# Weight loads: a list that shares both DMA queues by the packet, and a sixth place for raw weights

## The chip, the cores and the metric

The kernel runs on one core of one Trainium2 chip. The metric is device time in microseconds (us) of one execution; a profile of one execution comes from the hardware profiler.

## The reference, cut to what matters

```python
def swiglu(x, w_in, w_out):
    gate, up = jnp.split(x @ w_in, 2, axis=-1)
    return (jax.nn.silu(gate) * up) @ w_out
...
for layer in range(DEPTH):                       # DEPTH = 2
    h = h + 0.5 * swiglu(rms_norm(h, ffn1_norm[layer]), ffn1_w_in[layer], ffn1_w_out[layer])
    hn = rms_norm(h, mix_norm[layer])
    # layer 0: stick-breaking attention; layer 1: sliding-window attention with sinks, on a shared K/V
    h = h + attention(hn) @ w_o
    h = h + 0.5 * swiglu(rms_norm(h, ffn2_norm[layer]), ffn2_w_in[layer], ffn2_w_out[layer])
return rms_norm(h, final_norm)
```

All arrays are float32. There are 256 tokens, the model width is 1024, and each of the four feed-forward nets (FFNs) has a hidden width of 2816, so that one FFN reads a w_in of 1024 x 5632 and a w_out of 2816 x 1024. The weights are read once, and there are many of them for few tokens.

## The kernel before, in words

A float32 product is made from three cheaper ones: each operand is split into a high part, rounded to the type fp32r, and the remainder. For weights this is `split` (L419, L421): ScalarE (ACT) writes w_hi by a copy, and VectorE (DVE) writes w_lo = raw - w_hi, in two pieces of 128 x 1024 for each weight tile of 1 MB. TensorE (PE) then takes w_hi twice and w_lo once (`step`, `mm` L288). The operands on the other side are called xT (the normed stream), S (sums of quarters of it) and aT (the hidden activations) in the names that follow.

Tiles of raw weights live in five places (`RAWS = 5`) of a ring called `RAW`. A load into a place can only start when the last reader of the weights before it, mostly a w_lo on DVE, is done. All plain loads go through SyncE's queue (SP, L369), in order. The split halves live in ten places of `WP`.

An FFN is cut into blocks of hidden columns. Most of them (kind "s", `strassen`) compute the gate and up halves for both 128-token tiles with seven products in place of eight. Such a block loads four tiles r11, r12, r22 and r21, adds r12 and then r22 into r11 on DVE (L611), and has two more tiles added by the DMA engines themselves: `fetch` (L616) issues an accumulating transfer from GpSimd's queue (POOL), once into r12, and once into r11, after the product that uses r11 + r12 + r22 has been split. The last product of the block, on xT, needs this last fetch. Its gate result goes through a silu on ACT and a multiplication on DVE (L789, tile m), is transposed on PE (L677), and becomes aT. The w_out products of the block before (called out here) are done between the products of the block, and at the end of an FFN the products of the last two blocks follow one another.

No order is written by hand. The kernel builds a list of tasks with durations and dependencies (`Plan`), and `listed` runs through it engine by engine: among the tasks that are ready, each engine takes the one with the smallest priority. `due` works back from the end to give each task a due time, which is its priority in the next of four passes (PE keeps the given one), and the best pass sets the order of every engine's queue. In this model a plain load occupies SP for its bytes divided by 283 to 375 bytes per ns, one load after the other, and is usable 2000 ns later; a fetch takes 1500 ns of POOL, and SP for its bytes divided by 170.

Norm weights lie in two places `G4` of 512 KB. 8192 bytes are set aside as descriptor scratch of POOL's transfers.

Of the kernel before, what the change touches and what calls it, by code (L numbers as in the profile page):

```python
# [17 lines left out]
P = 128  # L18
# [19 lines left out]
PAIRS = 5  # L38
RAWS = 5
# [41 lines left out]
HEAD = 700.0  # L81
PASSES = 4
# [5 lines left out]
class Task:  # L88
    __slots__ = ("eng", "dur", "fn", "prio", "deps", "outs", "left", "ready", "start", "end", "seq", "lat")

    def __init__(self, eng, dur, fn, prio, seq, lat):
        self.lat = lat
# [23 lines left out]
class Plan:  # L116
# [3 lines left out]
    def add(self, eng, dur, fn, r=(), w=(), prio=None, lat=None):  # L120
# [19 lines left out]
        t.deps.discard(t)  # L140
        self.tasks.append(t)
        return t

    def lag(self, t, o):
        return t.lat if t.lat is not None else 0.0 if o.eng == t.eng and t.eng != "SP" else LAT[t.eng]

    def listed(self, prio):
        free = {e: HEAD for e in LAT}
        wait = {e: [] for e in LAT}
        queue = {e: [] for e in LAT}  # L150
        for t in self.tasks:
            t.ready, t.left = 0.0, len(t.deps)
            if t.left == 0:
                heapq.heappush(wait[t.eng], (t.ready, t.seq, t))
        done = []
        while True:
            best = None
            for e in LAT:
                if queue[e]:
                    at = free[e]  # L160
                elif wait[e]:
                    at = max(free[e], wait[e][0][0])
                else:
                    continue
                if best is None or at < best[0]:
                    best = (at, e)
            if best is None:
                break
            at, e = best
            while wait[e] and wait[e][0][0] <= at:  # L170
                t = heapq.heappop(wait[e])[2]
                heapq.heappush(queue[e], (prio[t.seq], t.seq, t))
            t = heapq.heappop(queue[e])[2]
            t.start = at
            free[e] = at + t.dur
            t.end = at + t.dur
            done.append(t)
            for o in t.outs:
                o.ready = max(o.ready, t.end + self.lag(t, o))
                o.left -= 1  # L180
                if o.left == 0:
                    heapq.heappush(wait[o.eng], (o.ready, o.seq, o))
        assert len(done) == len(self.tasks)
        return done, max(t.end for t in done)

    def due(self, done):
# [5 lines left out]
        for t in sorted(done, key=lambda t: (-t.start, -t.seq)):  # L192
            due[t.seq] = min([last.get(t.seq, 1e18)] + [due[o.seq] - self.lag(t, o) - t.dur for o in t.outs])
# [34 lines left out]
def kernel(  # L228
# [33 lines left out]

    RAW, WP, A4 = Slots("raw", RAWS, 8), Slots("w", 2 * PAIRS, 8), Slots("a", 4, 4)
    STG, S8, G4 = Slots("stg", 6, 3), Slots("s", 2, 8), Slots("g", 2, 4)
# [103 lines left out]
    def dma(src, dst, nbytes, w, prio, r=()):  # L368
        T("SP", nbytes / (283.0 if prio < -8.5e5 + 50 else 375.0 if prio < -8e5 else PLAIN), lambda: nc.sync.dma_start(out=dst(), in_=src), r=r, w=w, prio=prio)  # L369
# [245 lines left out]
    def fetch(dst, src):  # L615
        T("POOL", 1500, lambda: nc.gpsimd.dma_start(out=dst.ap, in_=src, accum_op=ALU.add), w=[(dst, 0), (dst, 1)],  # L616
          prio=plan.pos - LOADS, lat=500.0)
        T("SP", P * 2048 * 4 / ADDING, lambda: None, w=[(dst, 0), (dst, 1)], prio=plan.pos - LOADS)
# [9 lines left out]
    def ffn(w_in, w_out, acc, rest, finish, kv=None, blocks=BLOCKS, roots=None, ending=False, there=False, arranged=False):  # L628
# [145 lines left out]
        def strassen(n, c, between):  # L774
# [54 lines left out]
            if ORD[0] == "3":  # L829
                third()  # L830
            if not early:
                second(C11)
            if ORD[0] == "2":
                third()
            product(a, r11, of_s(1), False, False)
            fetch(r11, col(0, 1, c))
            u2 = stage(a, "u2")
            if ORD[0] == "6":
                third()
            plus(u2, d)  # L840
            mul_less(lambda: s1.ap, lambda: s1.ap, lambda: u2.ap, B(u2), B(s1), 0)
            STG.put(u2)
# [671 lines left out]
    def last(t, pair):  # L1514
# [44 lines left out]
        for j, c, ks in ((0, slice(0, 320), (0,)), (1, cuts[1], (640,)), (0, slice(320, 640), (0, 512))):  # L1559
# [8 lines left out]
            T(by, 500, lambda j=j, c=c, now=now, q=nc.scalar if by == "ACT" else nc.sync: q.dma_start(out=out[0, ts(t), c], in_=hg[j].ap[:, now]),  # L1568
              r=[(hg[j], ("to", c.start))], prio=1e9)
# [42 lines left out]
```

## Time and profile before

| What | Value |
|---|---|
| Median of 3 runs (lowest, highest) | 923.02 us (922.31, 923.92) |
| The profiled execution, and its span from first to last instruction | 924.5 us, 922.7 us |
| Mean granted TensorE clock | 0.997 |
| DMA | 214.43 MB, mean 232 GB/s |
| Plain loads of 1 MB of w_in from SP | 76, median 8.7 us from issue to landing |

The profile names a group of instructions by line, engine, and out<-in. PE is matmuls and PEld the loads of their stationary operand, which run one ahead of the matmuls. A row of waits says who waited, for whom, and then the total, the number and the longest wait in us. A row of windows gives, for one stretch, the length, and then the busy time of each engine with its number of instructions, the granted clock, the mean busy share of the 16 DMA engines, and GB/s. By time, the stages are: FFN 1 of layer 0 up to about 172 us, stick-breaking attention up to 300, FFN 2 of layer 0 up to 475, FFN 1 of layer 1 up to 660 (its last block from 620 on), sliding-window attention up to 740, and FFN 2 of layer 1 up to 905.

### The profile page before, as it was taken

The numbers are of one execution on the slowest core, as the hardware profiler recorded it, in microseconds if no ns is written. First come the engines' busy times: TensorE is split into PE (matmuls) and PEld (weight loads), VectorE is DVE, ScalarE is ACT, GpSimd is POOL, SyncE is SP. The second block draws the span as 40 slices with busy tenths as digits, with TensorE's granted clock in tenths as the row PEclk, the third lists the DMA queues.
The fourth block names the chain that finished last, engine by engine and source line by source line (L and its number), as shares of the span: only waits on it lengthen the run. The fifth ranks groups of instructions, "written<-read, shape, count | busy, mean of one in ns | idle before, by whom it ended". The sixth has DMA issues, their size and how long they took to land.

```text
span 922.7 us, 11848 instructions
## 1 busy us (share of the span) xinstructions
PE 905.2 (98%) x4420; PEld 739.5 (80%) x4420; DVE 816.6 (89%) x989; ACT 646.3 (70%) x935; POOL 66.8 (7%) x71
## 2 busy tenths in 40 slices
PE   9999999999999999999999999999999999999997
PEld 6888888788888877778788887887897787787776
DVE  8989898787967999898889999987789799999887
ACT  7867566777987865685588667755868676668563
POOL 2001010000000101010001001100000010001000
PEclk9999999999999999999999999999999999999999
DMA  9897999896752699989795999999843269998981
GB/s 336 302 255 191 299 300 244 260 267 190 242 183 92 138 272 273 242 261 258 206 337 156 246 255 260 288 280 244 305 151 115 92 146 259 303 230 250 302 220 46
DMA packets 107305, 214.43 MB, mean 232 GB/s; under 512 B 6256, under 2 KB 27760, under 8 KB 107248
## 3 DMA queue, kind: packets, MB, share of 16 engines
q1 hardware_dynamic: 85184, 170.49, 52.7%
q0 software_dynamic: 21648, 42.99, 27.1%
q8 instruction: 34, 0.56, 0.2%
q10 hardware_dynamic: 416, 0.20, 0.1%
q14 instruction: 23, 0.19, 0.1%
HBM read 212.62 MB, written 1.05 MB: 232 GB/s over the span
## 4 chain that ended last, share of the span: by engine, by line
PE 41%; DVE 24%; DMA 19%; issue 10%; ACT 6%; POOL 0%; ACTq 0%; POOLq 0%; DVEq 0%; SPq 0%
PE ps L288 38%; DMA raw<-in_ffn_w_in_dram 18%; DVE w_lo L421 15%; ACT w_hi L419 5%; DVE raw L611 4%; PE ps L491 1%; DVE aT_l L498 1%; PE ps L677 1%; PE ps L1346 1%; DMA raw<-in_ffn_w_out_dram 1%; DVE s L587 0%; DVE S_l L581 0%; DVE u L786 0%; DVE xT L498 0%; DVE p L786 0%
## 5 line engine op out<-in xcount | busy, mean ns | idle before, releaser
L421 DVE TENSOR_TENSOR w_lo<-raw,w_hi 128x1024 fp32r<-128x1024 f32 x424 | 498.3, 1217 | 52.9 <-ACT w_hi L419 51.7
L419 ACT CAST w_hi<-raw 128x1024 fp32r<-128x1024 f32 x424 | 424.4, 1050 | 141.5 <-DMA raw<-in_ffn_w_in_dram 69.8
L288 PE MATMUL ps<-w_hi,xT 128*128 128x512 f32 (+1 forms) x788 | 231.6, 378 | 1.9 <-ACT w_hi L419 1.8
L288 PEld LDWEIGHTS ps<-w_hi,xT 128*128 128x128 f32 x788 | 143.0, 190 | 28.9 <-ACT w_hi L419 2.9
L288 PE MATMUL ps<-w_lo,xT 128*128 128x512 f32 (+1 forms) x394 | 148.4, 377 | 2.1 <-DVE w_lo L421 2.0
L288 PE MATMUL ps<-w_hi,aT_h 128*128 128x512 f32 x354 | 140.0, 396 | 0.0
L288 PE MATMUL ps<-w_lo,aT_h 128*128 128x512 f32 x354 | 137.7, 389 | 0.0
L288 PE MATMUL ps<-w_hi,aT_l 128*128 128x512 f32 x354 | 137.4, 388 | 0.0
L288 PE MATMUL ps<-w_lo,S_h 128*128 128x512 f32 x320 | 126.1, 394 | 1.4 <-DVE w_lo L421 1.3
L288 PE MATMUL ps<-w_hi,S_h 128*128 128x512 f32 x320 | 126.2, 394 | 0.1
L288 PE MATMUL ps<-w_hi,S_l 128*128 128x512 f32 x320 | 124.7, 390 | 0.0
L611 DVE TENSOR_TENSOR raw<-raw 128x1024 f32<-128x1024 f32 x78 | 93.7, 1218 | 1.0 <-DMA raw<-in_ffn_w_in_dram 0.8
L288 PEld LDWEIGHTS ps<-w_lo,xT 128*128 128x128 f32 x394 | 74.5, 189 | 18.4 <-DVE w_lo L421 5.1
L616 POOL DMA_DIRECT2D raw<-in_ffn_w_in_dram x38 | 48.1, 1266 | 517.6 <-ACT w_hi L419 209.2
L288 PEld LDWEIGHTS ps<-w_lo,aT_h 128*128 128x128 f32 x354 | 66.5, 188 | 14.1
L288 PEld LDWEIGHTS ps<-w_hi,aT_l 128*128 128x128 f32 x354 | 66.6, 188 | 12.9
L288 PEld LDWEIGHTS ps<-w_hi,aT_h 128*128 128x128 f32 x354 | 66.5, 188 | 12.8
L288 PEld LDWEIGHTS ps<-w_lo,S_h 128*128 128x128 f32 x320 | 60.0, 188 | 18.6 <-DVE w_lo L421 6.2
L288 PEld LDWEIGHTS ps<-w_hi,S_h 128*128 128x128 f32 x320 | 60.1, 188 | 12.2 <-ACT u L782 0.5
L288 PEld LDWEIGHTS ps<-w_hi,S_l 128*128 128x128 f32 x320 | 60.1, 188 | 12.1
L497 ACT CAST aT_h<-ps 128x512 fp32r<-128x512 f32 (+1 forms) x48 | 26.3, 547 | 56.1 <-PE ps L677 56.1
L288 PE MATMUL ps<-xT,w_hi 128*128 128x512 f32 (+1 forms) x136 | 47.0, 395 | 0.0
(184 smaller groups left out, 942.3 us busy)
## 6 DMA issues: line engine op xcount, KB each, us to landing
raw<-in_ffn_w_in_dram SPq DMA_DIRECT2D x76, 1024.0 KB, 8.7
raw<-in_ffn_w_out_dram SPq DMA_DIRECT2D x44, 1024.0 KB, 6.4
raw<-in_ffn_w_in_dram POOLq DMA_DIRECT2D x38, 1024.0 KB, 9.3
raw<-in_sb_w_qkv_dram SPq DMA_DIRECT2D x12, 1024.0 KB, 8.8
raw<-in_ffn_w_in_dram SPq DMA_DIRECT2D x16, 512.0 KB, 6.6
raw<-in_ffn_w_in_dram SPq DMA_DIRECT2D x16, 256.0 KB, 5.5
raw<-in_sb_w_o_dram SPq DMA_DIRECT2D x4, 1024.0 KB, 5.7
raw<-in_swa_w_q_dram SPq DMA_DIRECT2D x4, 1024.0 KB, 9.1
```

Source lines behind the costliest of these rows:

```text
L288: PE.matmul(ps, lhsT=lhsT, rhs=rhs, start=start, stop=stop, skip_group_check=True)
L419: T("ACT", act(m), lambda sl=sl: ACT.copy(out=flat(hi)[:, sl], in_=flat(raw)[:, sl]), r=[(raw, i) for i in rs] + first, w=[(hi, i) for i i ...
L421: T("DVE", dve(m), lambda sl=sl: DVE.tensor_sub(out=flat(lo)[:, sl], in0=flat(raw)[:, sl], in1=flat(hi)[:, sl].bitcast(F32)), r=[(raw, i) ...
L491: PE.matmul(bank.ap[:, i * P:(i + 1) * P], lhsT=s, rhs=ident, start=i == 0, stop=True, is_transpose=True, skip_group_check=True)
L497: T("ACT", act(n), lambda: ACT.copy(out=hi[2](), in_=src()), r=B(bank), w=[hi[0:2]])
L498: T("DVE", dve(n), lambda: DVE.tensor_sub(out=lo[2](), in0=src(), in1=hi[2]().bitcast(F32)), r=B(bank) + [hi[0:2]], w=[lo[0:2]])
L611: T("DVE", dve(m), lambda sl=sl: DVE.tensor_add(out=flat(dst)[:, sl], in0=flat(dst)[:, sl], in1=flat(src)[:, sl]), r=[(src, k) for k in ks ...
L616: T("POOL", 1500, lambda: nc.gpsimd.dma_start(out=dst.ap, in_=src, accum_op=ALU.add), w=[(dst, 0), (dst, 1)], prio=plan.pos - LOADS, lat=5 ...
L677: PE.transpose(out=tr.ap[:, i * P:(i + 1) * P], in_=m.ap[:, i * P:(i + 1) * P], identity=ident)
L1346: PE.matmul(z[par].ap[:, i_ * P:(i_ + 1) * P], lhsT=e.ap[:, par * 384 + c:par * 384 + c + P], rhs=ident, start=i_ == 0, stop=True, is_tran ...
```

## The change

The list now plays both DMA queues as queues of packets. A DMA task occupies its issuing engine for 500 ns (SP) or 1000 ns (POOL); 1200 or 1700 ns after its start its packets are in queue HW or SW; the heads of both queues share the 16 engines packet by packet, in proportion to the time of one packet; and a transfer ends 900 or 500 ns after its last packet. The packets' times are a table. `RAW` gets a sixth place of 8 KB per partition. 4 KB of that come from the norm weights (`G4` from two places to one), and 4 KB from the descriptor scratch (8192 to 4096 bytes). `SEED1` is False, so that the branch it guards is not taken; PAIRS = 5 becomes HL = 10, which is the same number of places.

```diff
-PAIRS = 5
-RAWS = 5
+HL = 10
+RAWS = 6
+SEED1 = False
...
+SETUP = {"HW": 1200.0, "SW": 1700.0}
+LANDS = {"HW": 900.0, "SW": 500.0}
+ISSUE = 500.0
+PACKET = {4096: 157.0, 2048: 84.0, 1024: 50.0}
+ADDED = 176.0
...
+        while events or queues["HW"] or queues["SW"]:
+            heads = {k: q[0] for k, q in queues.items() if q}
+            total = sum(h[2] for h in heads.values())
+            next_ = [(last + h[1] * total / h[2], k) for k, h in heads.items()]
...
+                    k, n, each = t.moves
+                    queues[k].append([t, n * each + (0.0 if heads else RAMP), each])
...
-    STG, S8, G4 = Slots("stg", 6, 3), Slots("s", 2, 8), Slots("g", 2, 4)
+    STG, S8, G4 = Slots("stg", 6, 3), Slots("s", 2, 8), Slots("g", 1, 4)
...
     def dma(src, dst, nbytes, w, prio, r=()):
-        T("SP", nbytes / (283.0 if prio < -8.5e5 + 50 else 375.0 if prio < -8e5 else PLAIN), lambda: nc.sync.dma_start(out=dst(), in_=src), r=r, w=w, prio=prio)
+        size = max(p for p in PACKET if p == 1024 or p <= 4 * src.shape[-1])
+        T("SP", ISSUE, lambda: nc.sync.dma_start(out=dst(), in_=src), r=r, w=w, prio=prio, moves=("HW", nbytes / size / 16, PACKET[size]))
...
     def fetch(dst, src):
-        T("POOL", 1500, lambda: nc.gpsimd.dma_start(out=dst.ap, in_=src, accum_op=ALU.add), w=[(dst, 0), (dst, 1)],
-          prio=plan.pos - LOADS, lat=500.0)
-        T("SP", P * 2048 * 4 / ADDING, lambda: None, w=[(dst, 0), (dst, 1)], prio=plan.pos - LOADS)
+        T("POOL", 1000, lambda: nc.gpsimd.dma_start(out=dst.ap, in_=src, accum_op=ALU.add), w=[(dst, 0), (dst, 1)],
+          prio=plan.pos - LOADS, moves=("SW", P * 2048 * 4 / 2048 / 16, ADDED))
...
-    nc = _bacc.Bacc("TRN2", target_bir_lowering=False, num_devices=1, dynamic_dma_scratch_size=8192)
+    nc = _bacc.Bacc("TRN2", target_bir_lowering=False, num_devices=1, dynamic_dma_scratch_size=4096)
```

The number of instructions of each kind on PE, DVE, ACT and POOL stays; their order moves. On DVE, this is the last block of FFN 2 of layer 0 before. raw_3427 is r11, raw_3491 r22, raw_3472 r21; m_3509 belongs to the block before, and the two rows of w_lo_3563 are the split after which the last fetch into r11 may be issued:

```order
L611 TENSOR_TENSOR raw_3427<-raw_3427,raw_3449 128x1024 x2
L421 TENSOR_TENSOR w_lo_3504<-raw_3427,w_hi_3494 128x1024 x2
L789 SCALAR_TENSOR_TENSOR m_3509<-p5_3329,small_67,m_3509 128x512
L421 TENSOR_TENSOR w_lo_3527<-raw_3472,w_hi_3515 128x1024
L611 TENSOR_TENSOR raw_3427<-raw_3427,raw_3491 128x1024
L421 TENSOR_TENSOR w_lo_3527<-raw_3472,w_hi_3515 128x1024
L611 TENSOR_TENSOR raw_3427<-raw_3427,raw_3491 128x1024
L421 TENSOR_TENSOR w_lo_3563<-raw_3427,w_hi_3551 128x1024
L421 TENSOR_TENSOR w_lo_3572<-raw_3491,w_hi_3536 128x1024
L421 TENSOR_TENSOR w_lo_3563<-raw_3427,w_hi_3551 128x1024
```

Before, that split ends seven instructions of 128 x 1024 behind m. The same place on DVE now, where raw_3298 is r11, raw_3371 r22, raw_3397 r21, and w_lo_3518 the split that frees r11 for the last fetch:

```order
L642 TENSOR_TENSOR raw_3298<-raw_3298,raw_3352 128x1024 x2
L452 TENSOR_TENSOR w_lo_3440<-raw_3088,w_hi_3424 128x1024
L452 TENSOR_TENSOR w_lo_3476<-raw_3298,w_hi_3460 128x1024 x2
L642 TENSOR_TENSOR raw_3298<-raw_3298,raw_3371 128x1024 x2
L529 TENSOR_TENSOR aT_l_3502<-ps_66,aT_h_3438 128x4x128
L452 TENSOR_TENSOR w_lo_3509<-raw_3397,w_hi_3474 128x1024
L452 TENSOR_TENSOR w_lo_3518<-raw_3298,w_hi_3507 128x1024 x2
L819 SCALAR_TENSOR_TENSOR m_3527<-p5_3344,small_67,m_3527 128x512
L452 TENSOR_TENSOR w_lo_3509<-raw_3397,w_hi_3474 128x1024
```

It now ends right ahead of m: m has moved behind the additions and the split. On PE, just ahead of the last product of the same block (w_hi_3668 with xT), before; the last nine of the out matmuls in front of it are shown, 15 more stand between them and the product on the fetched r12, and nine ahead of that product:

```order
L288 MATMUL ps_66<-w_hi_3577,aT_h_3422 128x512
L288 MATMUL ps_66<-w_hi_3577,aT_l_3433 128x512
L288 MATMUL ps_66<-w_lo_3599,aT_h_3422 128x512
L288 MATMUL ps_66<-w_hi_3577,aT_h_3422 128x512
L288 MATMUL ps_66<-w_hi_3577,aT_l_3433 128x512
L288 MATMUL ps_66<-w_lo_3599,aT_h_3422 128x512
L288 MATMUL ps_66<-w_hi_3577,aT_h_3422 128x512
L288 MATMUL ps_66<-w_hi_3577,aT_l_3433 128x512
L288 MATMUL ps_66<-w_lo_3599,aT_h_3422 128x512
L288 MATMUL ps_66<-w_hi_3668,xT_163 128x512 x2
```

So 33 out matmuls stood between the product on r11 + r12 + r22 with r22's own and the last one. PE at the same place now, from the last matmul of the product on the fetched r12 to the last product (w_hi_3636 with xT):

```order
L318 MATMUL ps_66<-w_lo_3569,S_h_2566 128x512
L707 MATMUL ps_66<-ident_68,s1_3595 128x128 x4
L318 MATMUL ps_66<-w_hi_3600,aT_h_3438 128x512
L318 MATMUL ps_66<-w_hi_3600,aT_l_3502 128x512
L318 MATMUL ps_66<-w_lo_3606,aT_h_3438 128x512
L318 MATMUL ps_66<-w_hi_3600,aT_h_3438 128x512
L318 MATMUL ps_66<-w_hi_3600,aT_l_3502 128x512
L318 MATMUL ps_66<-w_lo_3606,aT_h_3438 128x512
L318 MATMUL ps_66<-w_hi_3600,aT_h_3438 128x512
L318 MATMUL ps_66<-w_hi_3600,aT_l_3502 128x512
L318 MATMUL ps_66<-w_lo_3606,aT_h_3438 128x512
L318 MATMUL ps_66<-w_hi_3636,xT_176 128x512 x2
```

Nine out matmuls stand ahead of it, and the other 24 come after it. In the last block of the other FFNs the number goes from 18 to 9 (FFN 1 of layer 0), from 33 to 9 (FFN 1 of layer 1) and from 36 to 9 (FFN 2 of layer 1). SP loads the same tiles; in the opening the two halves of the second token tile of x come after the second and the third quarter tile of weights, where both came after the fourth.

More of the change, by code (lines that the diff above doesn't have):

```diff
@@ L140, in add @@
         t.deps.discard(t)
+        t.moves = moves
         self.tasks.append(t)
@@ L144, in lag, with at, begin, ended @@
     def lag(self, t, o):
-        return t.lat if t.lat is not None else 0.0 if o.eng == t.eng and t.eng != "SP" else LAT[t.eng]
+        return 0.0 if t.moves else t.lat if t.lat is not None else 0.0 if o.eng == t.eng else LAT[t.eng]
     def listed(self, prio):
         free = {e: HEAD for e in LAT}
-        wait = {e: [] for e in LAT}
-        queue = {e: [] for e in LAT}
+        ready = {e: [] for e in LAT}
+        events, made = [], [0]
+        queues, last, done = {"HW": deque(), "SW": deque()}, 0.0, []
+        def at(time, what, t):
+            made[0] += 1
+            heapq.heappush(events, (time, made[0], what, t))
+        def begin(e, now):
+            if ready[e] and free[e] <= now:
+                t = heapq.heappop(ready[e])[2]
+                t.start = now
+                free[e] = now + t.dur
+                done.append(t)
+                at(free[e], "free", t)
+                if t.moves:
+                    at(now + SETUP[t.moves[0]], "moves", t)
+                else:
+                    at(free[e], "end", t)
+        def ended(t, now):
+            t.end = now
+            for o in t.outs:
+                o.ready = max(o.ready, now + self.lag(t, o))
+                o.left -= 1
+                if o.left == 0:
+                    at(max(o.ready, HEAD), "ready", o)
         for t in self.tasks:
@@ L153, in listed @@
             if t.left == 0:
[L154 to L157, printed above, removed]
-            for e in LAT:
[L159 to L182, printed above, removed]
+                at(HEAD, "ready", t)
+        while events or queues["HW"] or queues["SW"]:
+            heads = {k: q[0] for k, q in queues.items() if q}
+            total = sum(h[2] for h in heads.values())
+            next_ = [(last + h[1] * total / h[2], k) for k, h in heads.items()]
+            over = min(next_) if next_ else (1e18, None)
+            now = min(over[0], events[0][0] if events else 1e18)
+            for h in heads.values():
+                h[1] -= (now - last) * h[2] / total
+            last = now
+            if over[0] <= now:
+                t = queues[over[1]].popleft()[0]
+                at(now + LANDS[over[1]], "end", t)
+                continue
+            while events and events[0][0] <= now:
+                _, _, what, t = heapq.heappop(events)
+                if what == "moves":
+                    k, n, each = t.moves
+                    queues[k].append([t, n * each + (0.0 if heads else RAMP), each])
+                elif what == "end":
+                    ended(t, now)
+                elif what == "ready":
+                    heapq.heappush(ready[t.eng], (prio[t.seq], t.seq, t))
+            for e in LAT:
+                begin(e, now)
         assert len(done) == len(self.tasks)
@@ L192, in due @@
         for t in sorted(done, key=lambda t: (-t.start, -t.seq)):
-            due[t.seq] = min([last.get(t.seq, 1e18)] + [due[o.seq] - self.lag(t, o) - t.dur for o in t.outs])
+            due[t.seq] = min([last.get(t.seq, 1e18)] + [due[o.seq] - self.lag(t, o) - (t.end - t.start) for o in t.outs])
         return due
@@ L828, in strassen @@
                 add(r12, r22)
-            if ORD[0] == "3":
-                third()
-            if not early:
+            seeded = SEED1 and not early
+            if not early and not seeded:
                 second(C11)
-            if ORD[0] == "2":
-                third()
             product(a, r11, of_s(1), False, False)
             fetch(r11, col(0, 1, c))
-            u2 = stage(a, "u2")
-            if ORD[0] == "6":
+            if seeded:
+                T("ACT", act(512), lambda: ACT.copy(out=d.ap, in_=a.ap), r=B(a), w=B(d), prio=plan.pos - STAGE)
+                second(C11)
                 third()
-            plus(u2, d)
+                u2 = d
+            else:
+                u2 = stage(a, "u2")
+                third()
+                plus(u2, d)
+                STG.put(u2)
             mul_less(lambda: s1.ap, lambda: s1.ap, lambda: u2.ap, B(u2), B(s1), 0)
-            STG.put(u2)
             if ORD[1] == "t":
```

13 lines of the change are left out of this document (7 added, 6 removed).

## The prediction, made before the changed kernel ran

> **What bounds the kernel now.** I read the busy times first, then how far PE falls short in each stage, then what it waits for, and last what those waits go back to.
>
> ```profile
> PE 905.2 (98%) x4420; PEld 739.5 (80%) x4420; DVE 816.6 (89%) x989; ACT 646.3 (70%) x935; POOL 66.8 (7%) x71
> ```
>
> PE is the bound, and no work is taken from it: what can be won is only the time in which it waits. The windows by stage say where that is (length, then PE, PEld, DVE, ACT, POOL, clock, DMA share, GB/s).
>
> ```profile
> 140.00:172.00 32.00, 31.58 (x146) 25.79 (x145) 26.58 (x27) 21.94 (x27) 1.22 (x1) 1.00 0.88 253
> 300.00:475.00 175.00, 172.23 (x768) 137.74 (x767) 158.76 (x169) 118.43 (x153) 14.38 (x11) 1.00 0.87 246
> 475.00:620.00 145.00, 144.46 (x658) 118.70 (x657) 137.55 (x153) 103.25 (x134) 12.17 (x11) 1.00 0.89 254
> 620.00:660.00 40.00, 38.23 (x166) 30.95 (x165) 31.37 (x31) 26.91 (x34) 1.70 (x2) 0.96 0.86 239
> 740.00:905.00 165.00, 161.66 (x723) 130.53 (x722) 152.46 (x157) 110.17 (x137) 13.34 (x11) 1.00 0.85 238
> ```
>
> Length less PE's busy time is a lower bound of the stalls (0.42, 2.77, 0.54, 1.77 and 3.34 us), since the drain of a matmul counts as busy. The waits of the weight loads, which run ahead of the matmuls, are an upper bound. Here they are for the five windows in turn (waiter, line waited for, total, number, longest):
>
> ```profile
> PEld ps L288 <- DVE w_lo L421: 0.8, 1, 0.8
> ...
> PEld ps L288 <- DVE w_lo L421: 5.4, 10, 1.0
> PEld ps L677 <- DVE m L789: 1.7, 2, 0.9
> PEld ps L288 <- ACT w_hi L419: 0.9, 1, 0.9
> PEld ps L677 <- DVE aT_l L498: 0.7, 3, 0.3
> ...
> PEld ps L677 <- DVE aT_l L498: 1.3, 2, 0.8
> ...
> PEld ps L288 <- ACT w_hi L419: 1.7, 1, 1.7
> PEld ps L288 <- DVE w_lo L421: 1.0, 1, 1.0
> ...
> PEld ps L288 <- DVE w_lo L421: 3.6, 6, 1.0
> PEld ps L677 <- DVE m L789: 2.7, 2, 1.5
> PEld ps L677 <- DVE aT_l L498: 1.1, 2, 0.8
> ```
>
> They add up to 0.8, 8.7, 1.3, 2.7 and 7.4 us. Halfway between the bounds I take 0.6, 5.7, 0.9, 2.2 and 5.4. The fourth window has a clock loss besides:
>
> ```profile
> 646.00:648.00 2.00, 1.47 (x5) 0.70 0.00 0
> 648.00:650.00 2.00, 2.00 (x6) 0.50 0.38 100
> ```
>
> At 0.70 and 0.50 of full speed these 4 us lose 0.6 + 1.0 = 1.6 us. The budget is 0.6 + 5.7 + 0.9 + 3.8 + 5.4 = 16.4 us. The two FFNs that follow an attention have most of it.
>
> What the late w_lo and m go back to: SP's own waits, and the chain of waits at two places.
>
> ```profile
> SPq L369 <- DVE w_lo L421: 674.7, 122, 15.8
> ...
> 347.44 10.12 DMA raw<-in_ffn_w_in_dram
> ...
> 442.67 12.99 DMA raw<-in_ffn_w_in_dram
> 455.68 1.06 ACT w_hi L419
> 456.76 1.24 DVE w_lo L421
> 458.04 5.98 PE ps L288 x25
> ```
>
> SP stands 674.7 us before loads whose place is not free, 5.5 us at a time. The load at 347.44 is on the chain from its issue to its landing, with no slack between. And at the end of an FFN the last fetch (442.67) takes 13 us, and ACT, DVE and PE follow it one after the other. The engines of the DMA are not full before an FFN starts:
>
> ```profile
> 260.00:280.00 20.00, 20.00 (x123) 16.73 (x122) 12.25 (x18) 15.14 (x25) 0.00 (x0) 1.00 0.32 108
> 300.00:320.00 20.00, 20.00 (x91) 16.50 (x90) 20.00 (x26) 15.76 (x25) 4.19 (x3) 1.00 0.58 124
> ```
>
> With the places taken, the share is 0.32 and 0.58, and later 0.87 over the FFN. So places, and not bandwidth, hold the loads back there.
>
> **The change part by part.** The sixth place. Each load may be issued one release earlier, about 5.5 us by SP's mean wait. PE's waits inside the blocks are at most 1.5 us, so a load that is earlier by even half of that covers them where it is the cause. Not each is: DVE is busy for 158.76 of 175 us and 152.46 of 165, and a late m or aT_l can also come from DVE's order. Of the two windows' 5.7 + 5.4, the ends of the FFNs take 1.3 (458.04 less the 456.74 at which w_hi is there) and 1.0 (the longest w_lo wait of the last window); 8.8 is left for the blocks. The bounds are 0 and 8.8; I take half, **-4.4**, since load and order share the blame and no row parts them. Loads that are no longer late leave DVE as the next to be late.
>
> The ends of the FFNs. The budget is 0.6 + 1.3 + 3.8 + 1.0 = 6.7. On DVE the split that frees r11 moves from behind seven instructions after m to right ahead of m:
>
> ```profile
> L421 DVE TENSOR_TENSOR w_lo<-raw,w_hi 128x1024 fp32r<-128x1024 f32 x424 | 498.3, 1217 | 52.9 <-ACT w_hi L419 51.7
> L419 ACT CAST w_hi<-raw 128x1024 fp32r<-128x1024 f32 x424 | 424.4, 1050 | 141.5 <-DMA raw<-in_ffn_w_in_dram 69.8
> ```
>
> That is 7 x 1.217 = 8.5 us earlier for the fetch, if the data are there. On PE the last product moves ahead of 24 out matmuls. Their pace is read from two matmuls of one kind that stand three apart:
>
> ```profile
> 375.56 0.39 PE L288 MATMUL ps<-w_lo,S_h 128*128 128x512 f32 x1
> ...
> 376.25 0.39 PE L288 MATMUL ps<-w_lo,S_h 128*128 128x512 f32 x1
> ```
>
> 0.69 / 3 = 0.23 us, so 24 x 0.23 = 5.5 us of cover is given up. The net is 3.0 us more room than before, against a lateness of 1.3 to 2.2 us. The bounds are the whole 6.7 won, and 5.5 lost at each of three ends and 9 x 0.23 = 2.1 at the first if nothing comes earlier. I take two thirds of the gain, **-4.5**, because 3.0 exceeds the lateness but the fetch may be slower (below).
>
> The order of m. It now stands behind two additions and a split that wait for r22. Any delay of those reaches the transposition on PE, which has four waits of 4.4 us in all in the rows above. I add two more of that mean, **+2.2**; the bounds are 0 and one such wait in each of 20 blocks, 22.
>
> Fewer norm-weight places cost nothing: a gain is loaded once per stage, over 80 us apart (300, 475, 660, 740 are the stages' borders), so the one place is free in time; if not, SP stands still and the loads behind it are late. The list's durations for SP change no instruction.
>
> ```profile
> 0.00:20.00 20.00, 19.07 (x82) 13.39 (x83) 16.63 (x39) 17.14 (x34) 5.98 (x18) 1.00 0.93 328
> ```
>
> The opening's order: the third and fourth quarter tile of weights come one and two loads of 256 KB later, at 328 GB/s 0.8 us each, and x as much earlier. Nothing else is at work then; I take 0, between -0.8 and +1.6.
>
> ```profile
> L616 POOL DMA_DIRECT2D raw<-in_ffn_w_in_dram x38 | 48.1, 1266 | 517.6 <-ACT w_hi L419 209.2
> raw<-in_ffn_w_in_dram POOLq DMA_DIRECT2D x38, 1024.0 KB, 9.3
> ...
> raw<-in_sb_w_qkv_dram POOLq DMA_DIRECT2D x3, 1024.0 KB, 9.0
> ...
> 431.89 1.28 POOL L616 DMA_DIRECT2D raw<-in_ffn_w_in_dram  x1 [18.72 <-ACT w_hi L419]
> 442.67 1.26 POOL L616 DMA_DIRECT2D raw<-in_ffn_w_in_dram  x1 [9.50 <-DVE w_lo L421]
> ```
>
> Half the scratch. POOL's issue of a fetch takes 1.27 us, as the first row has it, and the fetch lands after a median of 9.3. No row shows how many fetches the scratch holds. If not one, POOL would be held for a landing; between 0 and 9.3 us for each, hidden only while the room above lasts. 41 fetches (38 and 3) are issued some 10 us apart, as in the last two rows, so that one has nearly landed when the next is issued, and I take 0.
>
>
> The sum is -4.4 - 4.5 + 2.2 = **-6.7 us**: the span goes from 922.7 to 916.0. The profiled execution took 924.5 us, 1.8 over its span and 1.5 over the median of the runs, 923.02; the difference is put on the median, which gives 916.3 us.
>
> **How long a fetch takes beside plain loads** decides the ends.
>
> ```profile
> q1 hardware_dynamic: 85184, 170.49, 52.7%
> q0 software_dynamic: 21648, 42.99, 27.1%
> ```
>
> Over 16 engines and 922.7 us a packet of q0 (the fetches) takes 0.271 x 16 x 922.7 / 21648 = 185 ns and one of q1 91 ns. A fetch is 21648 / 41 = 528 packets, 33 for each engine: 6.1 us alone, and 33 x (185 + 91) = 9.1 us if each one has a plain packet beside it. The 13 us at 442.67 say that it is already not alone. [...]
>
> A second row bears on the price of a stall, PE's first matmul behind the fall of the clock:
>
> ```profile
> 645.50 0.73 PE L288 MATMUL ps<-w_hi,xT 128*128 128x512 f32 x2 [1.25 <-ACT w_hi L419]
> ```
>
> The clock fell after PE had stood for 1.25 us. [...]
>
> **The rivals.**
> A, more is won: 90% of the blocks' 8.8 and all 6.7 at the ends, no new waits: -14.6, 908. For it speaks that FFN 1 of layer 1 runs with 0.9 us of stalls on the same code; against it, that DVE is over 90% busy in the two stages.
>
> B, the fetch gets slower. One more plain tile in the queue is 512 packets of 2 KB, 32 for each engine, x 91 ns = 2.9 us, which is just the 3.0 us of new room. Then the 4.5 at the ends is not won, and half of the 4.4 in the blocks goes where r12's fetch is late: -2.2 + 2.2 = 0, 923. For it speaks the DMA share of 0.87; against it, that the earlier fetch finds fewer loads issued after it. That the sixth place does nothing, because DVE frees all places late, comes out at the same time.
>
> C, slower: the fetch does not come earlier, because r22's addition waits for its load as before, while PE's order has already given up the cover. The 5.5 us then stand open at three ends and 2.1 at the first, 18.6, and a clock loss of 1.6 behind each of three: 23.4, less the 4.4 in the blocks: 942 at the worst. It decides from the point where the fetch is less than about 4.9 us earlier rather than 8.5 (5.5, less the 2.2 of gain left elsewhere over three and a half ends). Half way, 2.7 us earlier, it is 9.3 - 4.4 + 2.2 = +7.1, 930. For it speaks that DVE stood 51.7 us for ACT and ACT 69.8 us for loads in the rows of w_lo and w_hi above; against it, that r22 is the load whose place is gained.
>
> **How the numbers follow.** A measurement of this kernel tells 0.2%, 1.8 us, from no change. My forecast (about 911 to 921) has 0.47, A 0.19, B with the change that does nothing 0.14, C 0.20. Faster is the first two, 0.66; same 0.14; slower 0.20. The predicted time is the forecast's, 916.3. The range runs from A's time, 908, to a little short of C's half-way case, 927, and leaves out about a tenth on each side. The gaining cases' own range is 908 to 921.
>
> **What would show it.** Right: SP's total wait for w_lo falls well below 674.7; the DMA share from 260 to 320 us rises; the w_lo waits of 5.4 and 3.6 us at least halve; the clock stays at 1.00 near 645; the last fetch of an FFN is issued before m of the block before, and PE finds its w_hi ready. Wrong: long waits of the last products on w_hi or w_lo at the four ends (C), fetches with landings above 13 us (B), more and longer waits of the transposition L677 for m (the +2.2 too small), or POOL's issue far above 1.27 us (the scratch).

## The result, and the profile after

The changed kernel takes 918.28 us (917.68 to 918.87) against 923.47 us of the kernel before beside it: a ratio of 0.9944, 95% interval 0.9927 to 0.9961. It is 5.2 us faster; the prediction said 6.7 us and 916.3. A second set of runs gave 0.9942 (0.9924 to 0.9961). The profiled execution has a span of 917.1 us, 5.6 us shorter than before.

The busy times of the kernel after, from its page: PE does the same 4420 instructions and is still the bound.

```profile
PE 901.1 (98%) x4420; PEld 742.1 (81%) x4420; DVE 816.9 (89%) x989; ACT 648.1 (71%) x935; POOL 63.7 (7%) x71
```

The windows by stage of the kernel after (length, then PE, PEld, DVE, ACT, POOL, clock, DMA share, GB/s) answer to those of the prediction:

```profile
140.00:172.00 32.00, 32.00 (x149) 26.50 (x148) 24.42 (x25) 20.65 (x26) 1.22 (x1) 1.00 1.01 313
300.00:475.00 175.00, 172.16 (x777) 141.56 (x777) 160.65 (x171) 122.07 (x158) 13.71 (x12) 0.99 0.89 253
475.00:620.00 145.00, 143.64 (x653) 118.11 (x652) 141.68 (x155) 106.24 (x135) 12.07 (x10) 1.00 0.87 251
620.00:660.00 40.00, 40.00 (x187) 33.05 (x186) 30.69 (x34) 28.85 (x38) 1.82 (x2) 1.00 0.90 283
740.00:905.00 165.00, 162.12 (x724) 132.38 (x723) 153.72 (x164) 108.66 (x134) 13.38 (x11) 0.99 0.82 229
```

At the two ends of FFNs that have windows of their own (140 to 172 and 620 to 660) PE has no idle time left, where 0.42 and 1.77 us stood before, and the clock near 645 is 1.00 instead of 0.96. But the FFNs after an attention (300 to 475, 740 to 905) show almost as much as before, 2.84 and 2.88 us, and 475 to 620 has more, 1.36 for 0.54. The waits of the whole run tell why (waiter, line waited for, total, number, longest). First the kernel before:

```profile
PEld ps L288 <- DVE w_lo L421: 11.3, 19, 1.0
PEld ps L677 <- DVE m L789: 4.8, 5, 1.5
PEld ps L288 <- ACT w_hi L419: 3.6, 5, 1.7
PE ps L288 <- DVE w_lo L421: 3.3, 8, 0.5
PE ps L677 <- DVE m L789: 2.6, 4, 1.1
PE ps L288 <- ACT w_hi L419: 1.8, 2, 1.2
```

Then the kernel after:

```profile
PEld ps L707 <- DVE m L819: 7.1, 3, 3.2
PE ps L707 <- DVE m L819: 5.9, 3, 2.7
PEld ps L318 <- DVE w_lo L452: 2.3, 6, 0.8
PEld ps L318 <- ACT w_hi L450: 0.4, 2, 0.2
PE ps L318 <- DVE w_lo L452: 0.3, 1, 0.3
```

Halfway between the waits of PE and of PEld, as the prediction read them, w_lo falls from 7.3 to 1.3 us and w_hi from 2.7 to 0.2, together -8.5. The transposition's wait for m rises from 3.7 to 6.5, +2.8, in only three places. Together that is -5.7, for the 5.6 us by which the span is shorter. Most of it isn't idle time of PE in the profile: span less busy time goes from 17.5 to 16.0 us, and the busy time itself from 905.2 to 901.1, which fits short waits that hide behind the drain of a matmul (one of 128x512 stands in the profile for 0.39 us, and the next starts 0.23 us after it). PE's timeline of the kernel after has the three waits for m:

```profile
402.01 0.66 PE L707 MATMUL ps<-ident,m 128*128 128x128 f32 x4 [2.74 <-DVE m L819]
...
589.38 0.66 PE L707 MATMUL ps<-ident,m 128*128 128x128 f32 x4 [1.19 <-DVE m L819]
...
839.34 0.66 PE L707 MATMUL ps<-ident,m 128*128 128x128 f32 x4 [1.92 <-DVE m L819]
```

Behind the first and the third the clock falls in this execution (windows of the kernel after, clock third from the end); behind the second it doesn't:

```profile
404.00:406.00 2.00, 2.00 (x7) 1.54 (x6) 2.00 (x3) 2.00 (x5) 1.26 (x1) 0.50 0.35 133
...
590.00:592.00 2.00, 2.00 (x11) 1.61 (x10) 2.00 (x3) 2.00 (x4) 0.00 (x0) 1.00 1.06 347
840.00:842.00 2.00, 2.00 (x7) 1.53 (x7) 2.00 (x3) 2.00 (x4) 0.00 (x0) 0.59 1.03 331
```

The record of the granted clock has half speed for 3.41 us each time, which is 1.7 us if all of it reached the end: 3.4 here, 1.7 near 645 before. Here the runs speak against that. The four executions of this kernel had mean clocks of 0.995, 0.996, 0.998 and 0.999 and spans of 917.1, 916.9, 916.1 and 915.9 us, so that 3.7 us of clock (0.004 of 917) came with 1.2 us of span. (In the 17 of the kernel before that ran beside the first parts, below, the two go together more nearly one for one, 1.03 us of span for each us of clock, with much scatter: a correlation of 0.64.) In the profile of the second set the three waits are there again (2.71, 1.39 and 1.83 us, and a fourth of 1.20), and only the first has a fall behind it; the mean clock is 0.997, for 0.995 in the first profile.

What m waits for is on the chain of waits of the kernel after (start, length, what; the rows left out are additions, splits and the gaps between them):

```profile
373.82 14.26 DMA raw<-in_ffn_w_in_dram
...
388.16 1.06 ACT w_hi L450
...
401.20 0.76 DVE m L819
...
402.01 0.66 PE ps L707 x4
```

A fetch takes 14.26 us, and m stands behind the split and the additions that wait for it. From here the question was: what part of the change brings what, and why do some fetches take 13 to 14 us where the median is 9.2?

### The profile page after: what moved, and what is told of

The parts are those of the page before. It is cut to its first block, busy times and chain, and to the rows that moved or that the text cites. A ratio compares the mean times of both kernels' runs of the same rounds, so it can differ in the third digit from the quotient of the medians.

```text
span 917.1 us, 11868 instructions
## 1 busy us (share of the span) xinstructions
PE 901.1 (98%) x4420; PEld 742.1 (81%) x4420; DVE 816.9 (89%) x989; ACT 648.1 (71%) x935; POOL 63.7 (7%) x71
## 4 chain that ended last, share of the span: by engine, by line
PE 67%; DVE 19%; DMA 7%; issue 6%; ACT 1%; POOLq 0%; POOL 0%; ACTq 0%; DVEq 0%
PE ps L318 63%; DVE w_lo L452 12%; DMA raw<-in_ffn_w_in_dram 7%; DVE raw L642 3%; PE ps L707 1%; PE ps L522 1%; DVE aT_l L529 1%; PE ps L1378 0%; ACT w_hi L450 0%; DVE s L618 0%; DVE S_l L612 0%; DVE m L819 0%; DVE xT L529 0%; DVE u L816 0%; DVE e L1370 0%
## 5 line engine op out<-in xcount | busy, mean ns | idle before, releaser
L318 PEld LDWEIGHTS ps<-w_hi,aT_h 128*128 128x128 f32 x354 | 66.5, 188 | 12.7
```

What stands on the lines that cost most here:

```text
L318: PE.matmul(ps, lhsT=lhsT, rhs=rhs, start=start, stop=stop, skip_group_check=True)
```

## The experiments

### The parts of the change alone

[The list alone]: the changed kernel with the old numbers.

```diff
-RAWS = 6
+RAWS = 5
-G4 = Slots("g", 1, 4)
+G4 = Slots("g", 2, 4)
-dynamic_dma_scratch_size=4096
+dynamic_dma_scratch_size=8192
```

> The new list with five places, two norm-weight buffers and 8 KB of scratch: the change without its sixth place. Theory 1 (mine: the stalls at the ends of the FFNs went because the list, with queues modelled packet by packet, issues the last fetch earlier; inside the blocks list and place share the gain): about half of the change's -5.2 us stays, 919 to 922, with the four ends as free of waits as with the change (PE's shortfall at 620 to 660 under 0.5 us) and most w_lo waits of 300 to 475 back. Theory 2 (the sixth place wins it all, the list is neutral): 923, with a shortfall of 1 to 2 us near 645 as before. Theory 3 (the list wins it all and the place is idle): 918.

Measured: 936.69 us, 1.0111 (1.0098 to 1.0125). It is slower than before, which no theory had. The waits for m are the largest group, and an end of an FFN is worse than before:

```profile
PEld ps L707 <- DVE m L819: 13.9, 8, 2.8
PE ps L707 <- DVE m L819: 10.9, 6, 2.4
```

```profile
458.59 0.73 PE L318 MATMUL ps<-w_hi,xT 128*128 128x512 f32 x2 [2.24 <-ACT w_hi L450]
```

The last fetch of this FFN is issued at 442.09, for 442.67 before. The FFN itself starts 2.1 us later in this run (the last matmul of the attention ends at 298.70 and not at 296.56), so that the fetch is 2.7 us earlier in its FFN; it lands 15.4 us later instead of 13.0, and PE waits 2.24 us for its w_hi. That is the half-way condition of the prediction's rival C, but C isn't what makes the run slow: PE stands still for 5.2 us at the four ends, 3.8 before, where C had put 9.3. Its waits for m rise from 2.6 us to 10.9. That is the mechanism of the prediction's third term, the order of m, and far more than its +2.2.

[The place alone]: the kernel before with the three numbers of the change.

```diff
-RAWS = 5
+RAWS = 6
-G4 = Slots("g", 2, 4)
+G4 = Slots("g", 1, 4)
-dynamic_dma_scratch_size=8192
+dynamic_dma_scratch_size=4096
```

> The kernel before with six places for raw weights, one norm-weight buffer and 4 KB of scratch: the place without the new model of the queues. The old model with six places still makes its own list, so the order can shift. Theory 1 (list and place share): 920 to 922; SP's waits for w_lo stay near 675 us in sum, the w_lo waits of PE in the blocks (11.3 us in all before) fall by half, the stalls at the ends (1.3 us near 645) stay. Theory 2 (the place wins it all): 918. Theory 3 (the place is idle or hurts by more loads beside the fetches): 923 to 926, with fetches that land later than the median of 9.3 us.

Measured: 925.59 us, 0.9999 (0.9986 to 1.0011), the time of theory 3. Its windows show two opposite effects:

```profile
140.00:172.00 32.00, 28.91 (x127) 23.54 (x127) 24.24 (x24) 20.24 (x25) 1.22 (x1) 0.95 0.87 256
300.00:475.00 175.00, 174.28 (x798) 143.66 (x796) 164.52 (x177) 125.31 (x164) 14.94 (x12) 1.00 0.87 247
620.00:660.00 40.00, 35.52 (x148) 28.06 (x147) 25.95 (x27) 25.38 (x33) 1.82 (x2) 0.91 0.88 261
```

In the blocks from 300 to 475 the idle time falls from 2.77 to 0.72 us. At two ends it rises from 0.42 and 1.77 to 3.09 and 4.48. One of these, from PE's timeline and then POOL's and SP's:

```profile
642.90 1.22 PE L288 MATMUL ps<-w_hi,xT 128*128 128x512 f32 x2 [3.63 <-ACT w_hi L419]
```

```profile
626.66 1.26 POOL L616 DMA_DIRECT2D raw<-in_ffn_w_in_dram  x1 [9.74 <-DVE w_lo L421]
```

```profile
627.46 0.37 SPq L369 DMA_DIRECT2D raw<-in_ffn_w_out_dram  x1
```

The fetch is issued at 626.66, SP issues a plain load 0.8 us behind it, and the fetch lands 15.1 us after its issue.

[What the place was taken from]: the kernel before, with one norm-weight buffer and 4 KB of scratch but five places. The order of the instructions is that of before.

> The kernel before with one norm-weight buffer and 4 KB of scratch, and five places as before: only what the sixth place was taken from. My theory: no price, 923 within 0.2%, with POOL's issue of a fetch at 1.27 us as before. Rival: one norm-weight buffer holds SP up at the stage borders or the smaller scratch holds POOL, 924 to 927, which the change then has to earn back; POOL's issue would be well above 1.27 us, or SP would show a wait for a norm-weight buffer.

Measured: 929.3 us, 1.0035 (1.0022 to 1.0048). There is a price, against my theory, though POOL's issue stays at 1.27 us. So the scratch was halved by itself:

```diff
-dynamic_dma_scratch_size=8192
+dynamic_dma_scratch_size=4096
```

> The kernel before with 4 KB of scratch for the descriptors and nothing else; the order of the instructions is the same. It parts the 0.35% by which one norm-weight buffer and half the scratch together were slower. If the scratch is the price: 1.002 to 1.005. If the norm-weight buffer is, or if the 0.35% is scatter between programs of one order: within 0.2% of before. My theory is the second: no row of POOL changed (1.27 us for the issue of a fetch).

Measured: 928.59 us, 1.0034 (1.0021 to 1.0047). The scratch is the whole price, about 3.1 us; the norm-weight buffer costs nothing. My theory falls again.

### m's place in the list

```diff
-TM = 1000.0
+TM = 3000.0
```

> The changed kernel with one number of the list altered: m, which the transposition on PE waits for, is due 3 us ahead of its use rather than 1, so that it moves ahead in DVE's list. Theory 1 (the three waits of 1.2 to 2.7 us for m at 402, 589 and 839, two of them with the clock at half speed behind them, come from m's place behind additions that wait for a late fetch): they go, and the time falls by 3 to 6 us, to 912 to 915. Theory 2 (m is late because the fetch of 14 us on its own chain is late, wherever m stands in the list): the waits stay near those places, within 0.2% of 918. Theory 3 (DVE's total is the limit, and an earlier m makes splits late): the m waits go, w_lo waits come in their place, 917 to 921.

Measured: 918.91 us, 0.9921 (0.9909 to 0.9934), whose interval overlaps that of the change. The waits for m shrink from 7.1 to 2.2 us (PEld), but two others of the same size come (PE's timeline):

```profile
403.83 0.73 PE L318 MATMUL ps<-w_hi,xT 128*128 128x512 f32 x2 [2.59 <-ACT ps L842]
...
887.99 1.19 PE L318 MATMUL ps<-w_hi,xT 128*128 128x512 f32 x2 [2.78 <-DVE p L816]
```

The time fits theories 2 and 3, and the waits fit neither. m's place is not the cause; who stands behind the late fetch changes, and the fetches stay late (four of 13.1 to 14.2 us).

### Telling the list that some fetches are late

In the trace the long fetches have one thing in common. Four fetches of the change last 13.0 to 14.3 us. Each has a plain load issued 0.8 us behind it into a queue that has just run empty; the list's own model gives these fetches 11.0. The list was given a rule for it, and the change was timed beside it:

```diff
+BEHIND = 2400.0
...
+                    if k == "SW" and t.seq not in late:
+                        begun = now
+                    if k == "HW" and not queues["HW"] and len(queues["SW"]) == 1 and now < begun + 900:
+                        fetch = queues["SW"].popleft()[0]
+                        late.add(fetch.seq)
+                        at(now + BEHIND, "moves", fetch)
+                        heads = {}
```

> The changed kernel as it is, timed on the same chip as the three below, so that they can be set against it. All theories: 0.990 to 0.997 of the kernel before, with the three waits of the transposition for m near 402, 589 and 839 us.

> The changed kernel with one rule more in the list: a fetch whose plain neighbour enters an empty queue within 0.9 us behind it starts 2.4 us later than the list believed (it then lasts 13.6 us there instead of 11.0, near the 13.0 to 14.3 us of the trace). Theory 1 (m is late on the chip because the list takes these fetches 2 to 3 us too short and puts m behind the additions that wait for them): the three waits for m near 402, 589 and 839 and the clock losses behind two of them go, 9 us at most, so 909 to 914. Theory 2 (DVE has no room in these blocks: an addition or a split is late instead of m): the waits change their names, 916 to 920.

Measured: the change 919.95 us, 0.9942; with the rule 912.74 us, 0.9867 (0.9849 to 0.9885). Theory 1 holds. Behind the opening no idle time of PE is over 0.72 us, and of the waits for m one of 0.7 us is left (PEld). The long fetches are still there, nine of 13.0 to 14.3 us for the change's four; the list only puts nothing behind them that PE waits for. The same rule with five places:

> The same rule in the list, with five places, two norm-weight buffers and 8 KB of scratch, to be set against the list alone (1.0111 of the kernel before). Theory 1 (the new list alone was slower since six of its fetches last 13 to 14 us where it believes 11, and m waits 1.8 to 2.4 us behind them): 920 to 928, no m wait over 1 us. Theory 2 (with five places any list of this kind is late, since the places come free too late): 932 or more, with waits for w_hi and w_lo instead. Between them: both have a part.

Measured: 932.79 us, 1.0076 (1.0057 to 1.0095). This is the time of theory 2: the rule takes a third of the loss away, and with five places the new list stays slower than the old one. The waits part the theories less well: PE's longest are for s (2.3 and 2.2 us), w_hi (2.2) and m (1.6).

### Holding the plain load back

Whether the neighbour is what makes the fetch late was tried on the chip itself. POOL writes one column of the place that the neighbour loads into, behind its issue of the fetch, and the load must wait for that. It leaves PE's order as it is in the change; under thirty rows of DVE and ACT move.

```diff
+        if raw.slot[1] in held:
+            held.remove(raw.slot[1])
+            T("POOL", 100, lambda: POOL.memset(raw.ap[:, 0, 0:1], 0.0), w=[(raw, 0), (raw, 1)], prio=plan.pos - LOADS)
...
             def third():
                 product(d, r22, of_s(3), False, True)
                 RAW.put(r22)
+                held.append(r22.slot[1])
```

> The changed kernel with the plain load that follows a fetch held back until POOL has issued the fetch (POOL writes one column of the load's place behind the fetch, and the load must wait for it). It acts on the engines of the DMA, the list's model stays. Theory 1 (the fetch is slow because a plain load that is issued 0.8 us behind it reaches the idle DMA engines first; the first packet of the fetch comes 3.5 to 4.2 us after its issue instead of 1.9 to 2.2): these fetches land 11 to 12 us after their issue instead of 13 to 14.3, and the m waits shrink by about 2 us each, 911 to 915. Theory 2 (the fetch is slow because of the packets that alternate with it, whoever is first): it still takes 13 us or more, and the held load is a further delay, 918 to 922.

Measured: 910.99 us, 0.9848 (0.983 to 0.9866), 0.9% better than the change. By chance one fetch is issued at the same 373.82 us in both kernels, so their rows can be laid side by side. First the change: POOL's issue of the fetch, SP's loads, what the queues moved from 374.0 to 377.2 us (packets, MB, share; q0 is the fetch's queue), and the time to its landing.

```profile
373.82 1.27 POOL L647 DMA_DIRECT2D raw<-in_ffn_w_in_dram  x1 [10.18 <-DVE w_lo L452]
...
374.61 2.60 SPq L400 DMA_DIRECT2D raw<-in_ffn_w_in_dram  x2
...
q1 hardware_dynamic: 98, 0.20, 37.5%
...
DMA to landing us min/median/max: 14.3/14.3/14.3
```

Then the kernel with the held load:

```profile
373.82 1.27 POOL L650 DMA_DIRECT2D raw<-in_ffn_w_in_dram  x1 [9.94 <-DVE w_lo L455]
...
375.23 1.98 SPq L400 DMA_DIRECT2D raw<-in_ffn_w_in_dram  x2
...
q0 software_dynamic: 77, 0.16, 41.8%
...
DMA to landing us min/median/max: 11.2/11.2/11.2
```

In the change the plain load goes 0.79 us behind the fetch, and in the 3.2 us not one packet of the fetch moves, only 98 plain ones. Held back by 0.62 us more, the plain load has moved none and the fetch 77. The fetch lands 3.1 us earlier; the other three long fetches, which landed after 13.0 to 13.8 us, land after 9.9 to 10.0. Theory 1 holds, and theory 2 is out. In the four long fetches of the change the first packet comes 3.5 to 3.9 us after the issue; in most others 1.9 to 2.3 (six take 2.4 to 5.3 us, behind loads that are already moving). The neighbour's own first packet comes 1.0 us after its issue, so 1.8 us after that of the fetch, just ahead of the fetch's 1.9.

Of the 3.1 us, 1.9 are the earlier start (first packet at 1.99 us for 3.86). The rest comes from the packets: the fetch now moves alone until the plain load's first packet at 5.09. The plain load pays for it and lands 12.4 us after the fetch's issue instead of 9.9. Two other causes are out. DVE has the same seven w_lo beside the fetch in both kernels, from 369.9 to 377.9 us. And POOL's write isn't needed: in the change itself, without it, the fetches at 314.62 and 431.72 have their next load 1.1 and 1.65 us behind them and start after 1.97 us. But 0.8 us is no rule: the fetch at 87.44 has a load 0.60 us behind it and still starts first, after 1.95 us. The window of the blocks in the kernel with the held load:

```profile
300.00:475.00 175.00, 174.90 (x800) 144.10 (x799) 164.62 (x178) 126.55 (x164) 14.79 (x18) 1.00 0.90 263
```

PE is idle for 0.10 us of the 175, where the change has 2.84.

### The held load with each part

The kernel before has ten fetches of 12.7 to 14.4 us, each with a load 0.8 us behind it, and nine of them overtaken by it, so the held load was put into it, into the list alone and into the place alone (the same edit each time). These three are less clean than the one above: the list counts POOL's write as a task and comes out differently, in the kernel before in over a tenth of PE's and DVE's places. So their gains are those of the held load and of the list that goes with it.

> The kernel before with the load that follows a fetch held back until POOL has issued the fetch, as in the changed kernel with the held load (0.9848 of the kernel before, against 0.9942 without it). Theory 1 (a plain load issued 0.8 us behind a fetch puts it off by 2 us whatever the list; before has nine such fetches of 12.7 to 14.4 us, three of them at the ends of FFNs): these land in 10 to 12 us, the stalls at the ends (3.9 us with the clock near 645) go, and the time falls by 4 to 8 us, 0.991 to 0.996. Theory 2 (the old list leaves room for late fetches, so that only the new list profits): within 0.2% of before.

> The list alone (five places, two norm-weight buffers, 8 KB of scratch; 1.0111 of before) with the held load. Theory 1 (the list alone was slower because eight of its fetches are put off by a load behind them): 0.996 to 1.003, without the m waits of 2 us. Theory 2 (with five places the loads themselves come too late for this list, as the list that was told of the late fetches suggests at 1.0076): 1.005 or more, with waits for w_hi, w_lo and s.

> The place alone (old list, six places, one norm-weight buffer, 4 KB of scratch; 0.9999 of before) with the held load. Theory 1 (the place alone brought nothing because the gain in the blocks was lost again at the ends, 3.2 and 3.8 us at 161 and 643, behind fetches of 14.6 and 15.1 us that a load behind them puts off): these two stalls shrink by 2 to 3 us each with the clock losses behind them, 0.988 to 0.993. Theory 2 (the old list needs the new model to use the place): 0.997 or more.

All ratios against the kernel before:

| | as it is | with the held load |
|---|---|---|
| before | 1 | 0.9858 (0.9843 to 0.9873) |
| list alone, five places | 1.0111 | 1.0088 (1.0068 to 1.0108) |
| place alone, old list | 0.9999 | 0.9820 (0.9806 to 0.9835) |
| both (the change) | 0.9944, 0.9942 | 0.9848 (0.983 to 0.9866) |

Before and the place alone follow theory 1, with more than was expected: 911.93 and 908.54 us. In the place alone with the held load no idle time of PE is left in the blocks from 300 to 475, and the waits for w_lo fall to 2.2 us (PEld):

```profile
300.00:475.00 175.00, 175.00 (x802) 144.90 (x801) 165.20 (x177) 126.15 (x164) 15.36 (x17) 1.00 0.89 258
```

It is the fastest of all these kernels, 1.2% ahead of the change, and it has no new list. Where the load is held, the new list wins nothing: at six places it is at 0.9848 for 0.9820, with intervals that overlap, and at five it costs 2.3%.

With five places the new list is not saved, and this run doesn't quite part the theories. Its waits for m do shrink (13.9 to 3.6 us, PEld), but it has a new one:

```profile
PEld ps L318 <- ACT w_hi L453: 12.2, 5, 4.4
```

```profile
878.80 1.27 POOL L650 DMA_DIRECT2D raw<-in_ffn_w_in_dram  x1 [8.15 <-issue]
```

```profile
879.40 0.37 SPq L400 DMA_DIRECT2D raw<-in_ffn_w_out_dram  x1
```

At the four ends another load, of w_out, follows the fetch by 0.6 us; it goes into another place and isn't held, and these four fetches take 16.1 to 17.3 us.

## Why the prediction was right, and where it was not

The sign, the size and the range held: -5.2 us for -6.7. Read as waits, the first two terms came to -8.5 for -8.9 and the third to +2.8 for +2.2. The steps did worse than the sum, and that it came so near is partly luck: the place alone brings nothing, the list alone loses 1.1%, and a price of some 3 us for the scratch was not in it.

**The sixth place, -4.4.** The gain in the blocks is there: the place alone takes 300 to 475 from 2.77 to 0.72 us, and the w_lo waits of the whole run fall from 11.3 to 2.3 us in the change. But the place alone is worth nothing in the end, since the ends give it back. Freed of the late fetches it is worth 0.9820 / 0.9858, about -3.5 us, with the scratch's price in it. "Load and order share the blame" was right; what I didn't see is that one without the other gives nothing or less.

**The ends, -4.5.** All four are free of stalls. PE's idle time there was 3.8 us before, and the clock's fall near 645 is worth at most 1.7 more, so that between 3.8 and 5.5 us were won; the budget of 6.7 lay above that, and the 4.5 was sized well. So was the net room. The fetch at 442.67 moved to 431.72, 10.95 us earlier, and PE uses it at 449.79 instead of 456.78, 6.99 earlier (0.9 of both is the FFN's own earlier start):

```profile
431.72 1.27 POOL L647 DMA_DIRECT2D raw<-in_ffn_w_in_dram  x1 [8.15 <-DVE w_lo L452]
```

```profile
449.79 0.39 PE L318 MATMUL ps<-w_hi,xT 128*128 128x512 f32 x1
```

That is 4.0 us more room, for the 3.0 of the prediction. The condition that I named, "if the data are there", holds with the sixth place only: in the list alone the fetch is 2.7 us earlier in its FFN, and here 10.0. And there is a part that I did not have: the change's next plain load follows 1.65 us behind this fetch and not 0.84, and it lands in 12.1 us instead of 13.0. With the held load the kernel before has no stall at 620 to 660 either, though DVE's order moves there too.

**The order of m, +2.2.** This is the term that was mis-sized. The mechanism, m behind additions that wait for a load, is the one that was named. The waits cost +2.8, and the two falls of the clock behind them at most 3.4 us more. By the four executions' spans about a third of a fall reaches the end, which makes it some 4 us in all (an estimate: 2.8 and a third of 3.4), 6.2 at the most. I took the mean of short waits, 1.1 us, where the three are 1.2 to 2.7 us on PE. The delay that reaches PE is that of a fetch that is 2 to 3 us later than the list believes (13.0 to 14.3 us for 11.0). At six places it stays at that; in the list alone the same mechanism costs PE 10.9 us of waits.

**The clock.** The fall near 645 did go with its gap of 1.25 us, as the trace of before said. It began at 646.81, 1.3 us after the matmul of 645.50, which I had put behind it. Each fall, this one and the two of the kernel after, has 0.50 for 3.41 us. How long PE must stand for one isn't shown: gaps of 1.25, 1.92 and 2.74 us had a fall behind them, and one of 1.19 us had none. In the second profile of the change the gap of 1.83 us, at the place of the 1.92, has none either.

**Half the scratch, 0.** Wrong: 1.0034, some 3.1 us, and not by the way that I bounded (POOL held for a landing; its issue stays at 1.27 us). Why is not settled. One place is seen. Before, the fetch at 147.41 has a plain load 0.85 us behind it and is still first; with half the scratch the load comes 0.80 us behind, and the fetch loses. These are the packets of the 3.4 us from 147.4 before, and then from 149.1 with half the scratch:

```profile
q0 software_dynamic: 48, 0.10, 37.5%
q1 hardware_dynamic: 11, 0.05, 8.4%
```

```profile
q1 hardware_dynamic: 53, 0.21, 41.3%
```

PE then stands 1.18 us at 163.98 for w_hi. That is one of several places where the two runs drift apart, 4.9 us at the end of the two profiles. The same shift is seen at all the long fetches: with half the scratch and the old order, in both runs of it, the plain load comes 0.79 to 0.81 us behind and not 0.83 to 0.86, and the first packets of the fetches come after 3.8 to 4.2 us and not after 3.2 to 3.8. The nine that were overtaken before land after 13.6 to 13.7 us in the mean, for 13.5. So the race with the plain load is a likely part of the price; how much of the 3.1 us it makes isn't shown, since no run has half the scratch, the old order and the load held back.

**The norm-weight buffer, 0, and the opening, 0:** right. One buffer and half the scratch cost what half the scratch costs (1.0035 and 1.0034), and the first 20 us have PE busy for 19.07 us in both kernels.

**The rivals.** C's condition is what the list meets without the place, though the time goes to m and not to the ends. B named the right resource and missed the main reason. The two queues do run at once; from 379 to 385 us of the changed kernel they moved nearly as many packets each,

```profile
q0 software_dynamic: 380, 0.78, 69.9%
q1 hardware_dynamic: 383, 0.75, 38.4%
```

and that slows a fetch as B says: 380 packets in 6 us here, and 99 in the one us from 430 to 431, when the fetch's queue is alone. But it was so before the change too (403 and 355 packets from 383 to 389 us). What made these four fetches 3.0 to 3.8 us longer than with the load held back is which queue starts first, and no row that I used had it, though the row of 442.67 with its 12.99 us was in the prediction.

**What was to show it.** Right: the w_lo waits more than halved, the clock near 645, the last fetch no longer behind m of the block before (it is issued at 431.72, 0.3 us into m, which starts at 431.42, and so not quite before m, as I had written; before it went 9.0 us after m's start at 433.62). The DMA share ahead of the FFN is split: 0.30 for 0.32 from 260 to 280 us, 0.63 for 0.58 from 300 to 320. Fetches above 13 us were to be a sign of B; there are four of 13.0 and more, but before there were eight. Wrong in sign: SP's wait for w_lo was to fall well below 674.7 us and is

```profile
SPq L400 <- DVE w_lo L452: 678.5, 136, 15.8
```

With one place more SP runs one load further ahead and then stands before the next place just as long; the sum of its waits says nothing on whether its loads are late. ACT's wait for the loads of w_in does: 69.8 us before, 31.9 after.

## What to carry to other kernels

When two DMA queues are released by neighbouring instructions, look in the trace at which one moves its first packet first: here a plain load 0.8 us behind an accumulating fetch put its landing off by 3.0 to 3.8 us in the changed kernel, and holding that load back for 0.6 us was worth more (1.4% on the old kernel, with the list that went with it; 0.9% on the changed one, in nearly the same order) than the 0.6% of the new list and the sixth place together. A list that is made from a model of the chip is only as good as its latest transfer: compare each modelled duration with the trace, not the median with the median. And try the parts of a change alone: here the place alone was worth nothing, the list alone cost 1.1%, and the two together gained 0.6%.

## What was not expected of the hardware

- The start of a fetch depends on its neighbour: first packets 1.9 to 2.3 us after its issue, or 3.2 to 4.3 over the runs where a plain load, issued 0.8 us behind it into an empty queue, is out first. Why the second in line loses about 2 us, and not one packet of about 0.1 us (the plain queue's mean is 0.09), is open, and so is why a few fetches with a load as close behind them start first all the same; the runs show that it is so.
- Half the scratch for descriptors costs 0.34% with the same order of instructions and the same 1.27 us for POOL's issue.
- In the profiles of the kernel before and of the change the granted clock falls to 0.50 for 3.41 us three times, and once more in the last 3 us of each of the two; behind the gap of 3.63 us in the place alone it is 0.91 over the 40 us from 620 to 660, 3.6 us lost. Whether a gap of 1.2 to 1.9 us has a fall behind it can't be read from the gap's length. In the four executions of the changed kernel about a third of the clock that was lost showed in the span (1.2 of 3.7 us).
